# Winograd block products in a decoder layer: the products of a pair summed inside three PSUM banks, neighbouring pairs interleaved, left factors split three products ahead

## The chip, the cores and the metric

The kernel runs on one core of one Trainium2 chip. The metric is the device time of one execution in microseconds; the time before is the median of three executions, 2488.87 us (2486.42 to 2490.97). Five engines work side by side, each through its own queue of instructions in order: PE (matrix products), DVE (vector operations), ACT (activations, copies and casts), POOL (GpSimd, elementwise here) and SP, which issues the DMAs. PE writes into PSUM, which is used in banks of 128 partitions by 512 f32.

## The reference

One layer of a decoder trunk, sequence 1024, width 1024, all in f32:

```python
h = rmsnorm(x, norm_mix)
u = h @ w_in            # dq dk dv | rq rk rv rg | lx ly | gates
od = rmsnorm(diff_attention(dq, dk, dv, lam), diff_subln) * (1 - lam_init)
o_r = silu(rg) * group_norm(retention(rq, rk, rv))
o_l = rg_lru_branch(lx, ...) * gelu(ly)      # conv of 4, two gates, a scan over time
g = sigmoid(gates)                           # three gates of 1024 channels
merged = g0*(od @ w_branch0) + g1*(o_r @ w_branch1) + g2*(o_l @ w_branch2)
x = x + merged @ w_out
x = x + cross_attention(rmsnorm(x), rmsnorm(mem))
x = x + square(relu(rmsnorm(x) @ mlp_w1)) @ mlp_w2
return rmsnorm(x)
```

## The kernel before

**Arithmetic.** Every f32 product is made of three PE products of a faster 32-bit format. An operand is a `Split`: `hi`, a cast by ACT (line 70), and `lo`, the rest, a subtraction by DVE or POOL (line 71). `mm3` (lines 59 to 61) then multiplies hi by hi, hi by lo and lo by hi into the same bank.

**Block products.** The large projections use Winograd's form for 2 x 2 blocks: seven products instead of eight. A *unit* is a [128, 1024] piece of weights, read as a left factor of two blocks; two units make a *pair*, a left factor of 2 x 2 blocks A11 A12 A21 A22, whose result is a block of 256 channels by 1024 rows. Of it come the left factors A11, A12, S4, A22, S1, S2, S3 (`left`, line 1067, four DVE subtractions or additions of 128x512 a pair), and of the activations the right factors B11, B21, B22, T4, T1, T2, T3 (T1 to T4 are kept in DRAM and loaded as *blocks* of [128, 4, 512], each in two halves that ACT and DVE or POOL split). Product k is 12 matmuls of 128x512 into one bank. The seven are combined by `product`: with P1 to P7 the banks, c11 = P2 + P1, u2 = P6 + P1, u3 = P7 + u2, c22 = P5 + u3, u4 = P5 + u2, c21 = P4 + u3, c12 = P3 + u4. A copy of P1 by ACT (line 1122) and seven DVE additions that read a bank (lines 1126, 1128, 1131 for the inner ones, `emit` for the four results) do that, with `t0` and `t1` in SBUF as places for the partial sums.

**Stages.** `h_products` (about 765 to 1302 us) makes 23 pairs with h, the normalised input: eight for the LRU (every second pair), four for retention's gate, eleven for the merge gates. Beside each second pair run the LRU's own steps: a convolution on DVE, two small gate products on PE, sigmoids, tanh, exp and sqrt on ACT, a product on POOL, a scan on DVE. Then three branches (1302 to about 1556 us) of four pairs each, whose results are multiplied by the gates (`sgb`, loaded and put through a sigmoid by ACT) and added to what the branch before left in DRAM (`pv`). While the last two pairs of a branch run, the right factors of the next are loaded into the places that come free. After w_out and the cross-attention, `mlp_in` (about 1820 to 2144 us) makes 16 pairs with a squared ReLU on each result and sums for the next product, and `mlp_out` ends the layer.

**Order.** The Tile framework puts each engine's instructions into an order by the program's text and their dependencies. The text's order of products within a pair is `ORDER` or, where the right factors are still arriving, `BY_BLOCK` with two pairs side by side:

```python
ORDER = (1, 2, 6, 7, 5, 4, 3)
BY_BLOCK = (1, 2, 3, 7, 6, 5, 4)
```

A unit is cast and its low part subtracted where its product stands in the text; four weight tiles (two units each) let this run ahead. Low parts go to POOL, in the branches to DVE for products 6 and 4. PSUM has two banks for general use (`ps`) and six that rotate through the block products.

## Time and profile before

| | us |
|---|---|
| median of three executions | 2488.87 |
| the profiled execution: span | 2489.1 |
| PE busy in it | 2355.3 |
| DVE, ACT, POOL busy | 1851.9, 1042.4, 1088.3 |

The page gives no other time for the profiled execution than its span, which lies 0.2 us above the median. A matmul's row in the trace shows when it starts, how long it took and, in brackets, how long PE had been idle before it and which instruction ended the wait; the releaser named is the instruction whose signal came last. A busy PE is not always PE at full speed: PEclk is the granted clock, 1.00 at full speed.

### The profile page before, as it was taken

What the parts mean: (1) busy time and instruction counts of PE and PEld (TensorE: products, weight loads), DVE (VectorE), ACT (ScalarE), POOL (GpSimd) and SP (SyncE); (2) the same over time, 40 slices, a digit from 0 to 9 for tenths busy, and PEclk for the clock granted to TensorE, in tenths of its full rate; (3) what the DMA queues carried; (4) which work ended last, traced back from release to release, by engine and by line L of the source; (5) the groups of instructions that cost most, each with busy time, mean ns of one, the idle gap of its engine ahead of it and who ended that gap; (6) DMA issues with size and microseconds to landing.
All of it is one profiled execution on the core that took longest, in us unless ns stands there. A gap on an engine that the chain in (4) does not pass through costs nothing. (4 is left out here: it accounts for less than half of the span.)

```text
span 2489.1 us, 31236 instructions
## 1 busy us (share of the span) xinstructions
PE 2355.3 (95%) x11132; PEld 1906.0 (77%) x11132; DVE 1851.9 (74%) x2850; ACT 1042.4 (42%) x1823; POOL 1088.3 (44%) x714
## 2 busy tenths in 40 slices
PE   9999999999999999999998978899989999999996
PEld 7888878787876877777776767688768888778884
DVE  7577476767786777777677887534788888878888
ACT  5443344545455554454354443235442222343333
POOL 1122212221214555565553333225145555698787
PEclk9999999999999999999999989999999999999999
DMA  5222212122114435534576776434225444744432
GB/s 173 74 85 69 62 45 60 44 60 54 51 41 140 152 120 185 182 119 144 194 233 220 241 264 205 141 129 136 94 85 178 148 140 140 275 152 169 147 142 75
DMA packets 137259, 334.08 MB, mean 134 GB/s; under 512 B 17152, under 2 KB 27393, under 8 KB 137104
## 3 DMA queue, kind: packets, MB, share of 16 engines
q1 hardware_dynamic: 136528, 330.25, 40.2%
q8 instruction: 89, 1.46, 0.3%
q10 hardware_dynamic: 576, 1.84, 0.2%
q14 instruction: 66, 0.54, 0.1%
HBM read 229.21 MB, written 98.63 MB: 132 GB/s over the span
## 5 line engine op out<-in xcount | busy, mean ns | idle before, releaser
L59 PE MATMUL ps<-block,wu 128*128 128x512 f32 x1428 | 570.5, 400 | 55.6 <-DVE sf L1126 23.5
L61 PE MATMUL ps<-block,wu 128*128 128x512 f32 x1428 | 568.2, 398 | 16.7 <-POOL wu L71 10.2
L60 PE MATMUL ps<-block,wu 128*128 128x512 f32 x1428 | 565.0, 396 | 0.1
L71 POOL TENSOR_TENSOR wu<-st,wu 128x512 fp32r<-128x512 f32 x214 | 324.9, 1533 | 323.4 <-ACT wu L70 323.3
L59 PEld LDWEIGHTS ps<-block,wu 128*128 128x128 f32 x1428 | 273.2, 191 | 120.0 <-issue 19.6
L61 PEld LDWEIGHTS ps<-block,wu 128*128 128x128 f32 x1428 | 272.9, 191 | 85.5 <-POOL wu L71 15.8
L60 PEld LDWEIGHTS ps<-block,wu 128*128 128x128 f32 x1428 | 272.7, 191 | 60.7 <-DVE block L71 1.1
L70 ACT CAST wu<-st 128x512 fp32r<-128x512 f32 x240 | 141.5, 618 | 163.3 <-DVE st L1067 68.9
L59 PE MATMUL ps<-wu,hu 128*128 128x512 f32 x448 | 176.6, 394 | 15.6 <-DVE acc L1199 13.6
L71 POOL TENSOR_TENSOR w<-st,w 128x1024 fp32r<-128x1024 f32 x50 | 122.1, 2453 | 154.9 <-ACT w L70 137.5
L61 PE MATMUL ps<-wu,hu 128*128 128x512 f32 x448 | 174.9, 392 | 5.1 <-DVE hu L71 5.1
L60 PE MATMUL ps<-wu,hu 128*128 128x512 f32 x448 | 175.2, 391 | 0.1
L1199 DVE TENSOR_TENSOR acc<-acc,ps 128x512 f32<-128x512 f32 x216 | 137.8, 677 | 21.3 <-PE ps L61 20.6
L71 POOL TENSOR_TENSOR wu<-sf,wu 128x512 fp32r<-128x512 f32 x63 | 115.9, 1853 | 64.9 <-ACT wu L70 51.8
L71 DVE TENSOR_TENSOR hu<-sth,hu 128x1024 fp32r<-128x1024 f32 x56 | 122.1, 2185 | 20.6 <-ACT hu L70 20.2
L467 ACT ACTIVATE p<-sc,mx 128x256 f32<-128x256 f32 (+7 forms) x128 | 94.5, 740 | 65.8 <-DVE mx L464 61.9
L59 PEld LDWEIGHTS ps<-wu,hu 128*128 128x128 f32 x448 | 84.6, 189 | 38.9 <-DVE acc L1199 10.7
L59 PE MATMUL psk<-block,w 128*128 128x512 f32 x256 | 104.8, 409 | 0.0
L61 PEld LDWEIGHTS ps<-wu,hu 128*128 128x128 f32 x448 | 84.6, 189 | 23.5 <-DVE hu L71 6.0
L61 PE MATMUL psk<-block,w 128*128 128x512 f32 x256 | 101.8, 398 | 0.0
L60 PE MATMUL psk<-block,w 128*128 128x512 f32 x256 | 101.6, 397 | 0.0
L60 PEld LDWEIGHTS ps<-wu,hu 128*128 128x128 f32 x448 | 84.6, 189 | 17.8 <-POOL wu L71 0.5
(391 smaller groups left out, 5627.2 us busy)
## 6 DMA issues: line engine op xcount, KB each, us to landing
sth<-h SPq DMA_DIRECT2D x56, 512.0 KB, 8.9
st<-in_w SPq DMA_DIRECT2D x32, 512.0 KB, 4.3
h<-hab SPq DMA_DIRECT2D x32, 512.0 KB, 2.8
w<-in_w SPq DMA_DIRECT2D x8, 2048.0 KB
sgb<-gsp SPq DMA_DIRECT2D x48, 256.0 KB, 4.3
gsp<-l SPq DMA_DIRECT2D x44, 256.0 KB, 3.1
acc<-y SPq DMA_DIRECT2D x40, 256.0 KB, 4.2
st<-in_w_br SPq DMA_DIRECT2D x18, 512.0 KB, 6.4
```

What stands on the lines that cost most here:

```text
L59: nc.tensor.matmul(ps, lhsT=lhs.hi, rhs=rhs.hi, start=start, stop=False)
L60: nc.tensor.matmul(ps, lhsT=lhs.hi, rhs=rhs.lo, start=False, stop=False)
L61: nc.tensor.matmul(ps, lhsT=lhs.lo, rhs=rhs.hi, start=False, stop=stop)
L70: ins = self.nc.scalar.copy(dst.hi, src)
L71: self.lo_ins = (lo_engine or self.nc.vector).tensor_tensor(dst.lo, src, f32(dst.hi), op=ALU.subtract)
L467: nc.scalar.activation(p[:, 0:n], sc[:, 0:n], AF.Exp, bias=mx, accum_out=l)
L1199: eng.tensor_tensor(acc[k][:, st, :], acc[k][:, st, :], x if isinstance(x, bass.AP) else acc[x][:, st, :], op=ALU.add)
```

## The change

Three banks serve a pair: X for products 1 and 2, Y for 6, 7 and 4, Z for 5 and 3. A product can start on top of what its bank holds (`onto`: no matmul of it carries `start`). So c11 stands in X after product 2, c21 in Y after product 4 and c12, less one term, in Z after product 3. What is still added by other engines: DVE adds `t0` into bank Y in place after product 6 (u2), ACT copies that to `t0`, ACT copies Y after product 7 to `t1` (u3), and DVE makes c22 = Z + t1 and, at the end, c12 = Z + t0. Results that need no addition are taken from the bank by ACT (Copy, Gelu, Silu, or Relu and Square) or, in the branches, by the DVE multiplication with the gate.

`SLOT` interleaves neighbouring pairs: on PE the products follow one another as 6, 2, 5, 7, then 1 of the next pair, 4, 3, then 6 of the next pair. `play` makes a product's left factor (cast, low part, left sums) three products before it, with the low parts on GpSimd except in the first two pairs of the MLP, which keep the old form as `product_apart`. The left sums are made in place (S2 over A11, S3 over A21, S4 over A12). The two LRU gate products now come after products 4 and 3 of the following pair, both in the `ps` banks. In the branches the addition of `pv` goes from DVE to GpSimd. The right factors are loaded in another order: in `h_products` T2, T1, T3, T4 instead of T3, T2, T1, T4, with T2 needed after product 2 of the first two pairs (before, T3 after their product 3).

```diff
-    ORDER = (1, 2, 6, 7, 5, 4, 3)
-    BY_BLOCK = (1, 2, 3, 7, 6, 5, 4)
+    ORDER = (1, 6, 2, 5, 7, 4, 3)
+    SLOT = {1: 0, 6: 3, 2: 4, 5: 5, 7: 6, 4: 8, 3: 9}
+    BANK = {1: "X", 2: "X", 6: "Y", 7: "Y", 4: "Y", 5: "Z", 3: "Z"}
+    def overlapped(self, pairs):
+        return [x[1:] for x in sorted((7 * p + s, p, k) for p in pairs for k, s in self.SLOT.items())]
+    def play(self, seq, prep, run, ahead=3):
+        for i in range(-ahead, len(seq)):
+            if i + ahead < len(seq):
+                prep(*seq[i + ahead])
+            if i >= 0:
+                run(*seq[i])
...
+    def left_part(self, k, c, eng):
+        w, tt = c["w"], lambda o, x, y, op: eng.tensor_tensor(o, x, y, op=op)
         if k == 1:
+            tt(c["s1"], w["A21"], w["A22"], ALU.add)
+            w["S1"], w["S2"], w["S3"] = c["s1"], w["A11"], w["A21"]
+            tt(w["S3"], w["A11"], w["A21"], ALU.subtract)
+            tt(w["S2"], c["s1"], w["A11"], ALU.subtract)
+        elif k == 2:
+            w["S4"] = w["A12"]
+            tt(w["S4"], w["A12"], w["S2"], ALU.subtract)
...
+    def prepare(self, k, c, lo):
+        c["u", k] = self.pair_unit(c["w"][self.LEFT[k]], lo)
+        self.left_part(k, c, self.nc.vector)
...
+    def product(self, k, c, right, psum, emit, apart=False):
         nc, v = self.nc, self.nc.vector
+        u, r, b = c["u", k], right[self.RIGHT[k]], self.BANK[k]
+        onto = b in c
+        if not onto:
+            c[b] = psum()
+        ps = c[b]
+        self.mmk(ps, [(u[:, kt, :], r[:, kt, :]) for kt in range(4)], onto)
+        t0, t1 = c["t"]
+        if k == 1:
+            nc.scalar.copy(t0, ps)
+            if apart:
+                del c[b]
+        elif k == 2:
+            emit(0, 0, ps, None if onto else t0)
+        elif k == 6:
+            v.tensor_tensor(ps, ps, t0, op=ALU.add)
+            nc.scalar.copy(t0, ps)
+        elif k == 7:
+            nc.scalar.copy(t1, ps)
+            emit(1, 1, c["Z"], t1)
+        elif k == 4:
+            emit(1, 0, ps, None)
+        elif k == 3:
+            emit(0, 1, ps, t0)
...
 # h_products
+        def prep(p, k):
+            load(p)
+            self.prepare(k, cs[p], nc.gpsimd)
+            if k == 6:
+                load(p + 1)
...
-                elif k == self.ORDER[6]:
-                    self.lru_gate(jobs[p - 1][1], cs[p - 1], sp, sps)
+                elif k in (4, 3):
+                    self.lru_gate(jobs[p - 1][1], cs[p - 1], sp, k == 3)
...
-        for i in (3, 2, 1, 4):
+        for i in (2, 1, 3, 4):
...
-        for k in self.BY_BLOCK[1:]:
-            for p in range(2):
-                run(p, k)
-        for p in range(2, m - 2):
-            for k in self.ORDER:
-                run(p, k)
+        self.play([(p, k) for k in (2, 6, 5, 7, 4, 3) for p in range(2)] + self.overlapped(range(2, m - 2)), prep, run)
...
 # branch
-            v.tensor_tensor(o, x, y, op=ALU.add)
-            v.tensor_tensor(o, o, sg, op=ALU.mult)
+            if y is not None:
+                z = x if (n % 2, j) == (0, 1) else o
+                v.tensor_tensor(z, x, y, op=ALU.add)
+                x = z
+            v.tensor_tensor(o, x, sg, op=ALU.mult)
             if order > 0:
-                v.tensor_tensor(o, o, pv, op=ALU.add)
+                nc.gpsimd.tensor_tensor(o, o, pv, op=ALU.add)
...
+        seq = self.overlapped(range(2))
+        seq.insert(seq.index((1, 4)), (2, 1))
+        self.play(seq + [(p, k) for k in self.ORDER for p in (2, 3) if (p, k) != (2, 1)], prep, run)
...
 # mlp_in, emit
+            if y is None:
+                nc.scalar.activation(o, x, AF.Relu)
+                nc.scalar.activation(o, o, AF.Square)
+            else:
+                tt(o, x, y)
+                v.scalar_tensor_tensor(o, o, 0.0, o, op0=ALU.max, op1=ALU.mult)
```

How the instructions move is seen best at three places.

**ACT in one of the LRU's cycles (the sixth of eight), first before, then of the change.** `r` and `g` are the gates; the tanh (line 636 before, 641 after) waits for POOL's product `xc`; exp is line 637 (642 after), sqrt 638 (643); `COPY sf<-ps` of line 1122 is the copy of P1, those of lines 1179 and 1181 are the copies of bank Y after products 6 and 7.

```order
L634 ACT_TABLE_LOAD
L634 ACTIVATE r<-psr,vec 128x512 x2
L634 ACTIVATE g<-psi,vec 128x512 x2
L70 CAST wu<-st 128x512 x2
L1122 COPY sf<-ps_10637 128x512
L636 ACTIVATE g<-r,sp_8517 128x1024
L70 CAST lw<-lws 128x256
L637 ACT_TABLE_LOAD
L637 ACTIVATE r<-r,spm_8518 128x1024
L638 ACT_TABLE_LOAD
L638 ACTIVATE g<-g 128x1024
```

```order
L637 ACTIVATE g<-psr,vec 128x512 x2
L72 CAST wu<-st 128x512 x2
L72 CAST lw<-lws 128x256
L641 ACTIVATE g<-r,sp_8607 128x1024
L72 CAST wu<-st 128x512
L642 ACT_TABLE_LOAD
L642 ACTIVATE r<-r,spm_8608 128x1024
L643 ACT_TABLE_LOAD
L643 ACTIVATE g<-g 128x1024
L1179 COPY sf<-ps_10602 128x512
```

In the sixth, seventh and eighth cycle of the change the copy of line 1179, which product 7 needs, stands behind the sqrt; in the five cycles before, it stands ahead of the tanh, and the copy of line 1181 stands behind the sqrt instead.

**DVE while the second branch's right factors arrive, first before, then of the change.** `block<-st` is the low part of a half block, `wu` that of a unit, `L1126` and `L1178` are u2.

```order
L71 TENSOR_TENSOR block<-st_12401,block 128x1024
L71 TENSOR_TENSOR block<-st_12405,block 128x1024
L71 TENSOR_TENSOR wu<-st,wu 128x512
L71 TENSOR_TENSOR block<-st_12449,block 128x1024
L71 TENSOR_TENSOR wu<-sf,wu 128x512
L71 TENSOR_TENSOR block<-st_12453,block 128x1024
L1067 TENSOR_TENSOR sf<-st 128x512
L1067 TENSOR_TENSOR st<-st 128x512
L1067 TENSOR_TENSOR st<-sf,st 128x512
L1126 TENSOR_TENSOR sf<-ps_12499,sf 128x512
```

```order
L73 TENSOR_TENSOR block<-st_12245,block 128x1024
L73 TENSOR_TENSOR block<-st_12249,block 128x1024
L1178 TENSOR_TENSOR ps_12257<-ps_12257,sf 128x512
L1178 TENSOR_TENSOR ps_12274<-ps_12274,sf 128x512
L73 TENSOR_TENSOR block<-st_12290,block 128x1024
L845 TENSOR_TENSOR y<-ps_12171,sgb 128x512
L73 TENSOR_TENSOR block<-st_12294,block 128x1024
```

u2 stood behind six half blocks of this load and now stands behind two; no low part of a unit is left between them.

**ACT at the same place, of the change.** The casts of the half blocks wait for their DMAs; product 4 of the last two pairs waits for the two copies of line 1181. Before, the only copies here were those of P1.

```order
L72 CAST block<-st_12340 128x1024
L72 CAST block<-st_12344 128x1024
L836 ACTIVATE sgb<-sgb 128x512 x2
L72 CAST block<-st_12380 128x1024
L1181 COPY sf<-ps_12257 128x512
L72 CAST block<-st_12384 128x1024
L1181 COPY sf<-ps_12274 128x512
```

The first copy stands behind the seventh half block of the load, the second behind the eighth.

More of the change, by code (lines that the diff above doesn't have):

```diff
@@ L688, in emit @@
                     g = self.gate_order[n + i]
-                    tt(o[:, 0:HB], x, y)
+                    out(o[:, 0:HB])
                     nc.sync.dma_start(self.gsp[g * P:(g + 1) * P, sl], o[:, 0:HB])
@@ L722, in h_products, with last @@
                 self.after("hdma", nc.sync.dma_start(st, self.hTs[i - 1][:, 2 * q:2 * q + 2, :]))
-                self.split(b[:, 2 * q:2 * q + 2, :], st, nc.gpsimd if q and i != 3 else v)
-        for k in self.BY_BLOCK[1:]:
-            for p in range(2):
-                run(p, k)
-        for p in range(2, m - 2):
-            for k in self.ORDER:
-                run(p, k)
-        tags = itertools.cycle("rg")
-        self.right, load = self.load_blocks(1, lambda: self.sp.tile([P, 2, HB], F32, tag=next(tags), name="sto"))
-        for k in self.BY_BLOCK:
-            for p in range(m - 2, m):
-                run(p, k)
-            next(load)
+                self.split(b[:, 2 * q:2 * q + 2, :], st, nc.gpsimd if q and i != 2 else v)
+        self.play([(p, k) for k in (2, 6, 5, 7, 4, 3) for p in range(2)] + self.overlapped(range(2, m - 2)), prep, run)
+        tags = itertools.cycle("rg")
+        self.right, blocks = self.load_blocks(1, lambda: self.sp.tile([P, 2, HB], F32, tag=next(tags), name="sto"))
+        def last(p, k):
+            run(p, k)
+            if p == m - 1:
+                next(blocks)
+        self.play([(p, k) for k in self.ORDER for p in range(m - 2, m)], prep, last)
+    SLOT = {1: 0, 6: 3, 2: 4, 5: 5, 7: 6, 4: 8, 3: 9}
[7 more added lines that the diff above has]
+                run(*seq[i])
     def p6(self, psum):
```

189 lines of the change are left out of this document (102 added, 87 removed).

## The prediction

> **What bounds the kernel now.** I read the engines' shares first, then PE's waits by stage, then the stages by windows, and only then single rows. The page's first part says that PE is busy nearly all the time:
>
> ```profile
> PE 2355.3 (95%) x11132; PEld 1906.0 (77%) x11132; DVE 1851.9 (74%) x2850; ACT 1042.4 (42%) x1823; POOL 1088.3 (44%) x714
> ```
>
> So 134 us of idle PE are all there is to win, beside matmuls that run at less than full clock. The windows (length, then busy time and count of PE, PEld, DVE, ACT, POOL, then the granted clock, the DMA share and GB/s) show where they lie: h_products, the branches, three stretches within those or their ends, and the MLP's first product.
>
> ```profile
> 804.00:1302.00 498.00, 471.62 (x2000) 379.06 (x1999) 369.26 (x403) 232.09 (x334) 285.43 (x181) 0.98 0.50 167
> 1302.00:1556.00 254.00, 222.13 (x930) 179.59 (x929) 203.91 (x249) 111.60 (x171) 87.83 (x56) 0.94 0.70 230
> 1434.00:1538.00 104.00, 88.03 (x365) 70.71 (x363) 86.14 (x106) 45.98 (x70) 34.19 (x21) 0.93 0.75 247
> 1920.00:2100.00 180.00, 180.00 (x787) 147.40 (x786) 151.07 (x177) 41.35 (x74) 100.05 (x66) 1.00 0.45 152
> 1290.00:1300.00 10.00, 10.00 (x45) 8.23 (x44) 7.34 (x7) 5.06 (x8) 3.10 (x3) 1.00 0.94 323
> ```
>
> PE idles 498.00 - 471.62 = 26.4 us in h_products and 254.00 - 222.13 = 31.9 us in the branches; in the MLP window, which uses the same block products, it never idles. PE's waits, first in h_products, then in the branches:
>
> ```profile
> PE ps L59 <- DVE sf L1131: 13.3, 6, 2.6
> PE ps L61 <- POOL wu L71: 9.6, 12, 1.7
> PE ps L59 <- DVE sf L1126: 2.7, 1, 2.7
> ...
> PE ps L59 <- DVE sf L1126: 20.8, 3, 10.2
> PE ps L59 <- ACT wx L70: 5.9, 1, 5.9
> ```
>
> Two things are late: DVE with the additions that empty a bank, and the low part of a left factor. One such wait, on PE and on DVE:
>
> ```profile
> 930.12 0.40 PE L61 MATMUL ps<-block,wu 128*128 128x512 f32 x1
> 933.13 0.47 PE L59 MATMUL ps<-block,wu 128*128 128x512 f32 x1 [2.61 <-DVE sf L1131]
> 933.81 0.63 PE L61 MATMUL ps<-block,wu 128*128 128x512 f32 x1
> 934.24 0.63 PE L59 MATMUL ps<-block,wu 128*128 128x512 f32 x1
> ```
>
> ```profile
> 926.85 3.38 DVE L641 TENSOR_TENSOR_SCAN g<-r,xc 128x1024 f32<-128x1024 f32 x1
> 932.30 0.68 DVE L1131 TENSOR_TENSOR sf<-ps,sf 128x512 f32<-128x512 f32 x1
> ```
>
> The LRU's scan stood ahead of the addition; the bank came free 2.6 us late, and the matmuls after it start 0.43 us apart. Undisturbed ones do this:
>
> ```profile
> 783.77 0.39 PE L59 MATMUL ps<-block,wu 128*128 128x512 f32 x1
> 788.98 0.39 PE L61 MATMUL ps<-block,wu 128*128 128x512 f32 x1
> 793.44 1.16 PE L59 MATMUL ps<-block,wu 128*128 128x512 f32 x2 [4.08 <-ACT block L70]
> ```
>
> The first two rows are the first and last of 24 matmuls: 5.21 / 23 = 0.2265 us from start to start, so a product of twelve takes 2.72 us. Summed over all such slow matmuls, the low clock costs 7.5 us in h_products and 8.0 in the branches, 1.2 us per long wait. In all 33.9 and 39.9 us are lost there.
>
> **The change part by part.** The sum is made against the profiled execution's 2489.1 us; the median is 0.2 less.
>
> *Opening of h_products.* The third row above is PE waiting for the first T block. Its load is issued where it was, but only products 1 and 2 of two pairs come ahead of it, not 1, 2 and 3: 2 x 2.72 = 5.4 us less cover. **+5.4** (0 if the load moves up with the shorter stage before it, 8 if the second block is late too).
>
> *Additions taken off DVE, low parts earlier.* Per pair four of seven additions at 0.68 us go, 2.7 us of a pair's 19; banks are held by pairs, but six of them serve two pairs, and a unit made three products ahead has 8.2 us for cast (0.62) and low part (1.55). The 33.9 us of waits in h_products should go. What comes is a chain inside bank Y. The durations:
>
> ```profile
> L71 POOL TENSOR_TENSOR wu<-st,wu 128x512 fp32r<-128x512 f32 x113 | 173.2, 1552 | 122.0 <-ACT wu L70 121.8
> L70 ACT CAST wu<-st 128x512 fp32r<-128x512 f32 x115 | 66.6, 618 | 69.1 <-DVE st L1067 55.6 <-PE ps L61 6.9 <-DMA st<-in_w_gate 6.5
> L635 POOL TENSOR_TENSOR xc<-g,xc 128x1024 f32<-128x1024 f32 x8 | 19.2, 2402 | 28.6 <-ACT g L634 28.6
> L1122 ACT COPY sf<-ps 128x512 f32<-128x512 f32 x22 | 12.9, 586 | 5.9 <-PE ps L61 5.9
> L637 ACT ACT_TABLE_LOAD x8 | 10.3, 1283 | 0.1
> L634 ACT ACTIVATE g<-psi,vec 128x512 f32<-128x512 f32 x16 | 10.1, 689 | 3.7 <-DMA oTs<-g 2.1 <-PE ps L61 1.7
> L637 ACT ACTIVATE r<-r,spm 128x1024 f32<-128x1024 f32 x8 | 9.2, 1154 | 0.1
> L636 ACT ACTIVATE g<-r,sp 128x1024 f32<-128x1024 f32 x8 | 9.2, 1153 | 9.4 <-POOL xc L635 9.4
> L638 ACT ACTIVATE g<-g 128x1024 f32<-128x1024 f32 x8 | 8.5, 1063 | 0.1
> ```
>
> Between 6 and 7 lie two products, 5.4 us, for DVE's addition and ACT's copy. The addition into a bank is not in the trace; below, it takes the 0.68 us of an addition that reads one, above, four times the in-place one over 128 columns:
>
> ```profile
> L462 DVE TENSOR_TENSOR sc<-sc,cm x128: 268/298/300, 304.9 to 758.9; 128x128 f32<-128x128 f32 x128
> ```
>
> that is 1.2 us; I take 0.68, whose shape is the same. With 0.59 for the copy the chain fits, unless an engine is held up. ACT is, once per LRU cycle. I count from the end of product 4. The gates' 12 matmuls with product 3 between end at 5.4, the last sigmoid at 6.1. In cycles six to eight the order puts one cast (6.7) and its low part (8.3) ahead of POOL's product (10.7); then tanh (11.9), a cast (12.5), table and exp (14.9), table and sqrt (17.3), and only then the copy (17.9). Product 7 could start at 5.4 + 3 x 2.72 = 13.6: it waits 4.3 us and loses 1.2 to the clock, 5.5 x 3 = **16.5**. In the other five the copy after 6 is ahead of the tanh, and POOL's product has no late low part ahead of it: it ends at 8.5, tanh at 9.7, table and Gelu at 11.6, sqrt at 16.3, the copy after 7 at 16.9, with 19.0 allowed. That holds with 2.1 us to spare; I charge 1 each, **5**, since POOL may be in the middle of a low part. At the last pairs ACT also casts the first branch's half blocks, as it does between branches:
>
> ```profile
> 1336.38 2.00 ACT L70 CAST block<-st 128x1024 fp32r<-128x1024 f32 x2
> 1357.57 1.04 ACT L70 CAST block<-st 128x1024 fp32r<-128x1024 f32 x1 [2.55 <-DMA st<-oTs]
> 1360.63 1.05 ACT L70 CAST block<-st 128x1024 fp32r<-128x1024 f32 x1 [1.49 <-DMA st<-oTs]
> ```
>
> These are half blocks 1 and 2, 7 and 8. The first can start 5.4 us into the last two pairs (after both products 1); the seventh is then cast at 26.6, the copy of line 1181 behind it ends at 28.2, and product 4 could start after ten products, at 27.2; the eighth delays the second copy by another 0.4: **1.4**. So h_products: -33.9 + 16.5 + 5 + 1.4 = **-11.0** (-29 if only the 5 come, +11 if all eight cycles are late).
>
> *Branches.* The 39.9 us go as far as DVE causes them: u2 stood behind six half blocks, now behind two, and DVE gives up the `pv` additions and the low parts of products 6 and 4. Whether the gate's multiplication from a bank is cheaper, the next rows tell (min/median/max):
>
> ```profile
> L810 DVE TENSOR_TENSOR y<-ps,sf x48: 673/678/692, 1302.2 to 1569.5; 128x512 f32<-128x512 f32 x48
> L811 DVE TENSOR_TENSOR y<-y,sgb x48: 674/681/2875, 1305.3 to 1573.5; 128x512 f32<-128x512 f32 x48
> ```
>
> With a bank as one input it never takes more than 0.69; with two in SBUF up to 2.9. The Trainium skill, "SBUF — State Buffer", section "Who interferes with whom", says why: DVE with two SBUF inputs and GpSimd reading SBUF exclude each other for a whole instruction. These rows agree. The same rule speaks against the change, as it gives GpSimd more to read in SBUF while the left sums stay on DVE; by it the sum would lose some tenths of a us for each such sum, hidden where DVE has time.
>
> POOL's addition of `pv` is not in the trace: half of line 635's 2.40 below, 1.55 above; I take 1.3, so that a branch asks 28 x 1.55 + 16 x 1.3 = 64 us of POOL's 76. Hidden, just. What remains:
> - the wait for `wx` (5.9 and 1.6 of clock), which the change doesn't touch: 7.5;
> - DMA. The middle branch moves 48 pieces of 256 KB and 22 of 512 KB (sizes as the page's last part has them):
>
> ```profile
> sgb<-gsp SPq DMA_DIRECT2D x48, 256.0 KB, 4.3
> acc<-y SPq DMA_DIRECT2D x40, 256.0 KB, 4.2
> st<-in_w_br SPq DMA_DIRECT2D x18, 512.0 KB, 6.4
> ```
>
> that is 24.1 MB in 28 x 2.72 = 76.2 us of PE. Midway between the 247 GB/s of the windows and their 323 at best it takes 84.6: 8.4;
> - two more loads of blocks, 1.4 each: 2.8;
> - copies behind a sigmoid that waits for its `sgb` (63.5 us in 29 waits, 2.2 each, under one product's 2.72):
>
> ```profile
> ACT sgb L805 <- DMA sgb<-gsp: 63.5, 29, 6.9
> ```
>
> A few exceed it; I take 4.
>
> Together 22.7, so **-17.2** (-32 with the `wx` wait alone, +5 where a copy of each pair waits 2.2).
>
> *The rest.* At w_out the blocks last needed now come by way of POOL's additions: 0 (-5 to +5). In the MLP the order puts the end of one pair (an addition of 0.68, a square and a difference) and two left sums ahead of u2 and its copy. At the duration of the square before,
>
> ```profile
> L1155 DVE SCALAR_TENSOR_TENSOR hab<-hab 128x512 f32<-128x512 f32 x63 | 66.1, 1050 | 1.3
> ```
>
> for each of these four, that is 0.68 + 4 x 1.05 + 0.68 + 0.59 = 6.2 us against the 8.2 between products 3 and 7: **+1** (0 to +8). The squares moved to ACT cost nothing there: ACT is busy 41 of 180 us, and without that cover each is 1 us.
>
> Sum: 2489.1 + 5.4 - 11.0 - 17.2 + 1 = **2467**.
>
> **The rivals.**
> *Nearly all of it comes* (0.20). The chains fit everywhere but in cycles six to eight: 2489.1 - 33.9 + 16.5 - 39.9 + 7.5 + 5.4 = **2445**. For it: the MLP window shows these products without a wait. Against it: its ACT has nothing else to do.
>
> *ACT becomes the bound* (0.24), the case on the other side. Bank Y lets PE in only after ACT's copies, and ACT works in order. If all eight LRU cycles lose 5.5 us and one copy of each of the twelve branch pairs waits 2.2, h_products loses 44 + 1.4 - 33.9 = 11.5 and the branches 7.5 + 8.4 + 2.8 + 26.4 - 39.9 = 5.2: 2489.1 + 5.4 + 11.5 + 5.2 + 1 = **2512**. It decides from about 4 us a cycle, if the branches gain nothing. The Trainium skill, "PSUM — Partial Sum Buffer", section "PSUM bank collisions raise a hardware error", speaks for it: accesses of different engines to one bank have to be put one after the other, reads too. The waits of L59 on line 1131 agree for PE and DVE; three engines taking turns in one bank no row here shows.
>
> *DMA holds the branches* (0.18). At the 247 GB/s of the window above the middle branch takes 97.6 us, and the branches keep their 39.9: 2489.1 + 5.4 - 11.0 + 1 = **2484**, no change.
>
> The forecast has 0.38. **Chances:** a difference under 0.2%, 5 us, can't be told from none. Faster: 0.36 of the forecast, 0.20, and 0.06 of the DMA case, 0.62; the same 0.12, mostly the DMA case; slower 0.26. The range of 2440 to 2503 leaves out the tails of the second and third case, a tenth on each side; the forecast's own is 2455 to 2482.
>
> **What would show it.** Opening: the first wait on a T block near 9.5 us. h_products: no wait on line 1178 or on a low part; three waits of some 4 us of the `onto` matmuls on ACT's copies. Branches: PE's wait for `wx` left, DVE's long ones gone, GB/s near 285. Wrong would be the forecast if ACT's copies head PE's list of waits, or if DVE's left sums, now waiting for POOL's low parts, hold up u2.

## The result, and the profile after

The changed kernel takes 2550.92 us (median of four runs, 2549.82 to 2551.91) against 2487.64 us for the kernel before on the same chip: a ratio of 1.0257 [1.0242, 1.0271]. It is **slower by 2.6%**, where 2467 us were forecast. Its profiled execution spans 2549.6 us, 60.5 more than the one before. The engines' shares of the kernel after:

```profile
PE 2377.0 (93%) x11132; PEld 1918.0 (75%) x11132; DVE 1683.7 (66%) x2572; ACT 1155.0 (45%) x2016; POOL 1143.5 (45%) x770
```

DVE gave up 168 us of work, as the change says, and the number of matmuls is the same. PE still idles 39 us more, and its busy time rose by 22 us, which for equal matmuls points to more of them at the lower clock. To see where, I cut both traces at the same events: ACT's copy of P1 of the third, the 23rd and the 24th pair (the 24th is the first pair of the branches), the first matmul of w_out, the first of `mlp_out`, and the end of the span. All stage times below are cut this way, in us, from one trace of each kernel; where no edit touches a stage, two traces differ by up to 1.7 between the third and the 23rd pair, and by up to 4.2 in the branches (255.7 to 259.9 in seven versions with the same branches).

| | to the third pair | third to 23rd | 23rd to 24th | branches | w_out to `mlp_in` | `mlp_out` |
|---|---|---|---|---|---|---|
| before | 826.3 | 422.5 | 41.9 | 265.5 | 587.5 | 345.4 |
| after | 829.2 | 470.3 | 46.0 | 278.6 | 588.3 | 337.1 |
| difference | +2.9 | +47.8 | +4.1 | +13.1 | +0.8 | -8.3 |

So two stages lose and one gains. PE's waits over the whole kernel after, the longest of that list first:

```profile
PE ps L59 <- ACT sf L1179: 38.3, 10, 7.4
PE ps L59 <- ACT sf L1181: 31.2, 14, 7.2
PE ps L59 <- DVE acc L1293: 14.3, 10, 3.3
PE ps L59 <- ACT sf L1172: 13.6, 4, 6.7
```

Line 1179 is ACT's copy of bank Y after product 6 (product 7 may not start before it), line 1181 the copy after product 7 (product 4 waits for it), line 1172 the copy of P1 (product 2 waits for it). ACT's copies head the list, which the prediction had named as a sign that it is wrong. The windows of the two stages that lose, before:

```profile
826.00:1249.00 423.00, 399.31 (x1684) 319.93 (x1684) 310.38 (x342) 197.65 (x285) 240.21 (x154) 0.98 0.46 154
1290.00:1556.00 266.00, 234.13 (x982) 189.46 (x981) 213.25 (x256) 118.63 (x180) 92.93 (x59) 0.94 0.71 235
```

and after:

```profile
829.00:1300.00 471.00, 415.34 (x1696) 330.73 (x1697) 284.29 (x263) 245.39 (x358) 244.11 (x158) 0.94 0.41 139
1345.00:1624.00 279.00, 242.72 (x984) 193.75 (x985) 155.83 (x159) 129.12 (x202) 158.77 (x108) 0.93 0.68 220
```

In h_products (the first row of each) PE idles 55.7 us instead of 23.7, and the granted clock falls from 0.98 to 0.94: 94 matmuls run at about half pace instead of 38, 20.0 us of extra time instead of 7.5. Idle 32.0 and clock 12.5 together are 44.5 of the 47.8. DMA moves less per second, not more, in both stages, so its rate isn't the bound. In the branches POOL is busy 158.8 us instead of 92.9.

**One wait in full.** In the kernel after, PE (the last matmul of product 5, then product 7 of the same pair):

```profile
1056.17 0.40 PE L61 MATMUL ps<-block,wu 128*128 128x512 f32 x1
1061.92 0.79 PE L59 MATMUL ps<-block,wu 128*128 128x512 f32 x1 [5.36 <-ACT sf L1179]
1062.51 0.63 PE L60 MATMUL ps<-block,wu 128*128 128x512 f32 x1
1062.94 0.63 PE L61 MATMUL ps<-block,wu 128*128 128x512 f32 x1
```

ACT, which had been idle for 2.54 us when its copy came:

```profile
1061.28 0.59 ACT L1179 COPY sf<-ps 128x512 f32<-128x512 f32 x1 [2.54 <-DVE ps L1178]
```

and DVE, ahead of its addition into the bank (line 1178, u2):

```profile
1047.34 3.38 DVE L646 TENSOR_TENSOR_SCAN g<-r,xc 128x1024 f32<-128x1024 f32 x1
1051.85 1.76 DVE L1125 TENSOR_TENSOR st<-sf,st 128x512 f32<-128x512 f32 x1 [1.12 <-POOL wu L73]
1053.54 1.75 DVE L647 TENSOR_TENSOR l<-l,g 128x1024 f32<-128x1024 f32 x1
1055.21 1.78 DVE L616 TENSOR_SCALAR xc<-lx,vec 128x1024 f32<-128x1024 f32 x1
1056.91 0.68 DVE L689 TENSOR_TENSOR l<-ps,sf 128x512 f32<-128x512 f32 x1
1057.51 1.27 DVE L618 SCALAR_TENSOR_TENSOR xc<-lx,vec,xc 128x1024 f32<-128x1024 f32 x1
1058.71 0.68 DVE L780 TENSOR_TENSOR r<-r 128x512 f32<-128x512 f32 x1
1059.31 1.27 DVE L618 SCALAR_TENSOR_TENSOR xc<-lx,vec,xc 128x1024 f32<-128x1024 f32 x1
1060.50 0.69 DVE L1178 TENSOR_TENSOR ps<-ps,sf 128x512 f32<-128x512 f32 x1
```

Product 6 had ended two products, 5.4 us, before product 5 did, so near 1051.1. Its addition began 9.4 us later. Before it stood a left sum that waited 1.12 us for POOL, the LRU's product, three steps of the next convolution, a result (line 689) and a sum for a branch's input (line 780): all of them DVE's own work in its own order. The addition took 0.69 us and the copy 0.59. ACT was not what was late here; it merely came last in the chain, and the list of waits names the last.

The chain is PE, DVE, ACT, PE, inside one bank, with 5.4 us of cover. Before, the same addition could be late by more, since it freed a bank of its own and PE had others to go on with.

**The eight waits taken apart.** In h_products PE waits eight times for line 1179, 33.1 us in all, once per LRU cycle. The first five, 29.1 us (4.9 to 7.4 each), are of the kind just shown: ACT had been idle before its copy until the addition ended, and the same left sum, product, convolution steps, result and branch sum stood ahead of the addition, which began 8.9 to 11.4 us after product 6. In cycles six to eight DVE is in time and ACT is late, as here in the sixth (PE, DVE, ACT):

```profile
1138.88 0.50 PE L59 MATMUL ps<-block,wu 128*128 128x512 f32 x1 [1.08 <-ACT sf L1179]
```

```profile
1131.41 0.70 DVE L1178 TENSOR_TENSOR ps<-ps,sf 128x512 f32<-128x512 f32 x1 [1.96 <-PE ps L61]
```

```profile
1137.30 1.06 ACT L643 ACTIVATE g<-g 128x1024 f32<-128x1024 f32 x1
1138.26 0.57 ACT L1179 COPY sf<-ps 128x512 f32<-128x512 f32 x1
```

The copy stands behind the sqrt and comes 6.1 us after the addition. These three waits are 1.1, 1.6 and 1.3 us, 4.0 in all. In the other five cycles PE also waits 0.7 to 1.2 us, 4.7 in all, for the copy of line 1181, again behind ACT's sqrt. So ACT is late where the prediction put it and costs little there; DVE is late where the prediction charged nothing.

### The profile page after: what moved, and what is told of

Same layout as the page of the kernel before. It is cut to its first block, busy times and chain, and to the rows that moved or that the text cites. A ratio compares the mean times of both kernels' runs of the same rounds, so it can differ in the third digit from the quotient of the medians.

```text
span 2549.6 us, 30999 instructions
## 1 busy us (share of the span) xinstructions
PE 2377.0 (93%) x11132; PEld 1918.0 (75%) x11132; DVE 1683.7 (66%) x2572; ACT 1155.0 (45%) x2016; POOL 1143.5 (45%) x770
## 5 line engine op out<-in xcount | busy, mean ns | idle before, releaser
L59 PE MATMUL ps<-block,wu 128*128 128x512 f32 x1428 | 583.3, 409 | 113.4 <-ACT sf L1179 38.3
L61 PE MATMUL ps<-block,wu 128*128 128x512 f32 x1428 | 573.8, 402 | 0.9 <-DVE wu L73 0.5
L60 PE MATMUL ps<-block,wu 128*128 128x512 f32 x1428 | 572.6, 401 | 0.0
L73 POOL TENSOR_TENSOR wu<-st,wu 128x512 fp32r<-128x512 f32 x232 | 353.3, 1533 | 360.3 <-ACT wu L72 348.7
L59 PEld LDWEIGHTS ps<-block,wu 128*128 128x128 f32 x1428 | 277.7, 195 | 190.4 <-ACT sf L1179 42.7
L61 PEld LDWEIGHTS ps<-block,wu 128*128 128x128 f32 x1428 | 277.4, 194 | 67.1 <-DVE wu L73 0.9
L60 PEld LDWEIGHTS ps<-block,wu 128*128 128x128 f32 x1428 | 278.1, 195 | 61.8 <-DVE block L73 0.8
L59 PE MATMUL ps<-wu,hu 128*128 128x512 f32 x448 | 176.1, 393 | 14.3 <-DVE acc L1293 14.3
L1125 DVE TENSOR_TENSOR st<-st 128x512 f32<-128x512 f32 x69 | 87.7, 1272 | 78.7 <-POOL wu L73 77.8
L73 POOL TENSOR_TENSOR wu<-sf,wu 128x512 fp32r<-128x512 f32 x69 | 108.8, 1584 | 45.6 <-ACT wu L72 34.0
L59 PEld LDWEIGHTS ps<-wu,hu 128*128 128x128 f32 x448 | 84.4, 188 | 36.2 <-DVE acc L1293 13.3
L61 PEld LDWEIGHTS ps<-wu,hu 128*128 128x128 f32 x448 | 84.6, 189 | 19.0 <-DVE hu L73 1.3
```

What stands on the lines that cost most here:

```text
L59: nc.tensor.matmul(ps, lhsT=lhs.hi, rhs=rhs.hi, start=start, stop=False, **kw)
L60: nc.tensor.matmul(ps, lhsT=lhs.hi, rhs=rhs.lo, start=False, stop=False, **kw)
L61: nc.tensor.matmul(ps, lhsT=lhs.lo, rhs=rhs.hi, start=False, stop=stop, **kw)
L73: self.lo_ins = (lo_engine or self.nc.vector).tensor_tensor(dst.lo, src, f32(dst.hi), op=ALU.subtract)
L1125: w, tt = c["w"], lambda o, x, y, op: eng.tensor_tensor(o, x, y, op=op)
```

## The experiments

Stage times of all runs (cut as above; the first column of the table above stayed within 826.1 and 831.0, that of w_out to `mlp_in` within 581.5 and 599.9, the longest in e1 to e4, whose edits reach the MLP too), with the ratio to the kernel before. "Own banks" means that no sum is made in a bank: every product has its own, and the additions are DVE's, as before.

| run | third to 23rd | 23rd to 24th | branches | `mlp_out` | ratio [95%] |
|---|---|---|---|---|---|
| before | 422.5 | 41.9 | 265.5 | 345.4 | 1 |
| after | 470.3 | 46.0 | 278.6 | 337.1 | 1.0257 [1.0242, 1.0271] |
| e1, own banks everywhere | 449.1 | 44.1 | 283.7 | 342.9 | 1.0230 [1.0188, 1.0272] |
| e2, bank Y alone undone | 461.7 | 42.5 | 282.7 | 335.3 | 1.0265 [1.0232, 1.0298] |
| e3, ACT's copies to DVE | 472.3 | 42.9 | 280.8 | 336.4 | 1.0273 [1.0233, 1.0314] |
| e4, factors one product ahead | 474.9 | 44.4 | 274.0 | 337.7 | 1.0281 [1.0248, 1.0314] |
| x8, before with the new MLP | 423.2 | 42.7 | 265.7 | 336.8 | 0.9964 [0.9946, 0.9982] |
| x5, gates as before, `pv` on DVE | 467.9 | 44.4 | 264.8 | 337.7 | 1.0158 [1.0128, 1.0187] |
| x6, x5 with own banks in h_products | 444.0 | 41.0 | 263.8 | 336.8 | 1.0049 [1.0027, 1.0072] |
| x7, x6 in the old order | 428.0 | 40.5 | 259.4 | 337.2 | 0.9947 [0.9916, 0.9979] |
| z2, after with one tap of the convolution | 464.5 | 43.9 | 279.6 | 337.9 | 1.0218 [1.0185, 1.0250] |
| y3, x6 with factors five ahead | 452.0 | 41.2 | 260.5 | 336.7 | 1.0051 [1.0031, 1.0071] |
| x9, x7 with before's h_products | 423.8 | 43.4 | 258.2 | 337.5 | 0.9939 [0.9918, 0.9960] |
| y7, x7 with the gates' input split earlier | 419.6 | 41.7 | 258.0 | 337.5 | 0.9923 [0.9899, 0.9948] |
| i1, y7 interleaved | 442.2 | 41.2 | 255.7 | 336.8 | 1.0007 [0.9996, 1.0017] |
| w1b, y7 with products 1, 6, 2, 7, 5, 4, 3 | 421.7 | 41.8 | 259.0 | 337.8 | 0.9943 [0.9921, 0.9966] |
| w1, w1b with the sums in banks | 452.5 | 42.4 | 259.0 | 337.9 | 1.0077 [1.0046, 1.0107] |
| w2, w1b with bank X's sum alone | 424.1 | 41.4 | 259.9 | 337.6 | 0.9942 [0.9925, 0.9958] |
| w3, after with `pv` on DVE | 468.6 | 45.8 | 262.1 | 337.6 | 1.0172 [1.0142, 1.0201] |
| w4, y7 with `pv` on GpSimd | 420.2 | 42.9 | 268.9 | 336.7 | 0.9964 [0.9947, 0.9981] |

### Parts undone in the changed kernel

Four runs undo one suspect each. e1 takes all sums out of the banks:

```diff
-            self.product(k, c, H, psum or self.p6(sps), emit, psum is not None)
+            self.product_apart(k, c, H, psum or self.p6(sps), emit)
```

(and the same in the branches and the MLP). 

> The change with every product in a bank of its own again and all sums made by DVE as before the change; order, interleaving, splitting three ahead and the additions on GpSimd stay. Theory A (the chain in one bank: product 6, DVE's addition, ACT's copy, product 7, ACT's copy, product 4 lets PE wait for the queues of DVE and ACT): the waits on those copies, 76 us in the block products, go, some of the old waits for a bank (16 to 24 us) come back; 2470 to 2500 us. Theory B (splitting ahead with the low parts on GpSimd and sums in place makes DVE wait and collide): DVE has even more to do, 2540 us or more. Theory C (weights loaded later, so that DVE waits for them): little moves, 2530 to 2560.

e2 gives products 7 and 4 banks of their own, so that only the chain of bank Y goes:

```diff
-    BANK = {1: "X", 2: "X", 6: "Y", 7: "Y", 4: "Y", 5: "Z", 3: "Z"}
+    BANK = {1: "X", 2: "X", 6: "Y", 7: "U", 4: "V", 5: "Z", 3: "Z"}
-            v.tensor_tensor(ps, ps, t0, op=ALU.add)
-            nc.scalar.copy(t0, ps)
+            v.tensor_tensor(t0, ps, t0, op=ALU.add)
-            nc.scalar.copy(t1, ps)
+            v.tensor_tensor(t1, ps, t0, op=ALU.add)
...
-            emit(1, 0, ps, None)
+            emit(1, 0, ps, t1)
```

> The change with bank Y alone undone: products 6, 7 and 4 have a bank each and DVE adds as before (u2, u3, c21); banks X and Z still sum in place. Theory A: as PE waits on nothing between 6, 7 and 4, nearly all of the 70 us of waits on the copies after 6 and 7 go, and DVE's load stays under that of before: 2460 to 2490 us. Theory B or C: 2530 us or more.

e3 leaves the chain and takes ACT's queue out of it, at the price of two more copies in DVE's queue:

```diff
-            nc.scalar.copy(t0, ps)
+            v.tensor_copy(t0, ps)
-            nc.scalar.copy(t1, ps)
+            v.tensor_copy(t1, ps)
```

> The change with the copies after products 6 and 7 made by DVE instead of ACT; everything else as it is. Theory A says which queue holds which copy: in the branches the copy after 7 waits behind ACT's sigmoids and casts that wait for DMAs (27 us of PE's waits there), and these go, in h_products the copy after 6 waits for DVE's addition behind the LRU's scan and convolution, and those 33 us stay: 2510 to 2535 us. If ACT's queue were the bound in both places, 2470 to 2490. If neither, 2550 or more.

e4 splits the left factors one product ahead instead of three (`ahead=1`). 

> The change with left factors split one product ahead instead of three. Theory A: the chain is unchanged and low parts come late again (10 us of waits before the change): 2550 to 2590 us. Theory B: DVE waits less for GpSimd between its sums, and the time falls to 2530 us or less.

Between the third and the 23rd pair e1 gave back 21.2 us, e2 8.6, e3 nothing (+2.0) and e4 nothing (+4.6). As whole kernels e1, e2 and e3 (2541.6, 2550.2 and 2552.2 us) stay above the ranges that theory A, the chain alone, gave them. The sums in the banks are part of the loss; the distance of three isn't. e3 alone doesn't clear ACT's queue: with the copies on DVE, PE waits 22.0 us for line 1181, where it was 4.7. That DVE and not ACT makes most of the waits shows in the eight taken apart above. e1 got less than half of what was lost, and its waits show why. PE's waits in h_products of e1:

```profile
PE psr L59 <- ACT r L637: 29.7, 6, 8.7
PE psr L60 <- DVE xcs L73: 8.3, 3, 4.1
```

With the bank chain gone, PE waits where it hadn't: for the LRU gates (`psr`), whose products the change had put at another place, and for the low part of their input. In the kernel after, these two waits hid behind the others. So one limit taken away at a time undercounts each, and I went on from the other end.

### The change taken apart, from the old kernel's side

x8 is the kernel before with the MLP's part of the change alone. x5 is the changed kernel with the LRU gates where they were and `pv` added by DVE; x6 is x5 with own banks in h_products (and the branches' low parts of products 6 and 4 on DVE again); x7 is x6 with the old order of products and loads and the split of the gates' input after product 4, where it stood, and in the branches own banks and all low parts on GpSimd. In short:

```diff
# x5, against the changed kernel
-                elif k in (4, 3):
-                    self.lru_gate(jobs[p - 1][1], cs[p - 1], sp, k == 3)
+                elif k == 3:
+                    self.lru_gate(jobs[p - 1][1], cs[p - 1], sp, sps)
-                nc.gpsimd.tensor_tensor(o, o, pv, op=ALU.add)
+                v.tensor_tensor(o, o, pv, op=ALU.add)
# x6, against x5
-            self.product(k, c, H, psum or self.p6(sps), emit, psum is not None)
+            self.product_apart(k, c, H, psum or self.p6(sps), emit)
-            self.prepare(k, cs[p], nc.gpsimd)
+            self.prepare(k, cs[p], v if k in (6, 4) else nc.gpsimd)
# x7, against x6
-    ORDER = (1, 6, 2, 5, 7, 4, 3)
+    ORDER = (1, 2, 6, 7, 5, 4, 3)
-        for i in (2, 1, 3, 4):
+        for i in (3, 2, 1, 4):
...
```

> Two edits of the change, in stages that the trace separates. In h_products the LRU's two gate products go back to where they were before the change (both after product 3, the second one's banks from the rotating six); the sums stay in the banks. In the branches the addition of pv goes back to DVE. Own banks took 21 us of the 52 lost in h_products, and then PE waited for the gates' products instead (38 us, for ACT's sigmoids and the low part of their input). Theory D (two limits that hide each other, the chain in bank Y and the gates' place): this edit alone moves h_products by less than 10 us. Theory E (the gates' place is the main loss, by making the LRU's own chain longer): it gives 25 us or more. Branches: if GpSimd's additions make its low parts late, 5 to 13 us come back; if the stream of blocks from DRAM is the limit, under 3 us.

> In h_products both are undone, the sums in the banks and the gates' place; the interleaving, the splitting three ahead and the left sums in place stay. Theory D: most of the loss goes, the stage of h_products is within 10 us of before. If it still loses 20 us or more, the interleaving or the splitting ahead is a cause of its own. In the branches the addition of pv is on DVE and the low parts of products 6 and 4 are on DVE, as before the change, with the sums in the banks: as in the run beside it, 5 to 13 us come back if GpSimd's load is the cause, under 3 us if it isn't.

> In h_products and the branches the order of products, the order of loads and the places of the gates and of the LRU's steps go back to before the change, each product has its own bank and pv is added by DVE; what is left of the change there is the splitting three products ahead with the left sums in place and all low parts on GpSimd. The MLP is that of the change. If the interleaving and the sums in the banks are the causes, both stages are back within 8 us of before, 2475 to 2492 us in all (the MLP's part gained 8). If splitting ahead is a cause, 2505 us or more.

> The kernel before with the change in the MLP's first product alone. In the change's trace the stages from w_out on took 8 us less than before, at the start of the MLP's second product, and the first product's own time is the same. If that gain belongs to the MLP's part: 2476 to 2483 us, that is 5 to 10 us faster than before. If it came from elsewhere, no change.

The gates' place is worth 2.4 us in h_products (470.3 to 467.9), hardly more than traces differ (w3, below, has the h_products of the kernel after and 468.6), the sums in banks 23.9 (x5 to x6), and the rest lies in x6 to x7, 16.0, where several edits stand together. x8 shows that the MLP's part is a gain by itself: h_products and the branches as before, `mlp_out` 8.6 us shorter. In the branches x5 and x6 stand at 264.8 and 263.8, so the low parts of products 6 and 4 matter no more there.

### Is it DVE's queue, and are the weights late?

If u2 is late because of what stands ahead of it on DVE, then less of that should help. z2 is the changed kernel with three of the four taps of the LRU's convolution left out (`range(1, 4)` to `range(1, 1)`), so part of the reference's work is missing there. 

> The change with three of the four taps of the LRU's convolution left out: eight times 3 x 1.3 = 3.9 us less on DVE, of which two taps (2.6 us) stand between the LRU's scan and the u2 addition into bank Y. Everything else is the change. Theory A' (in h_products PE's wait for the copy after product 6 is DVE's queue: scan, convolution, left sums ahead of u2): these eight waits, 33 us, shrink by 2.6 each and the slow matmuls after them with them; the stage from the third to the 23rd pair falls by 20 to 35 us, 2515 to 2532 in all. If ACT's queue or the gates set it, under 8 us: 2542 or more.

```profile
PE ps L59 <- ACT sf L1179: 20.6, 8, 4.4
PE ps L59 <- DVE lx L689: 10.4, 3, 4.9
PE psr L59 <- ACT r L637: 9.7, 3, 3.3
```

That is PE's list in h_products of z2. The first row was 33.1 us in eight waits in the kernel after, so 12.5 went, and all of it from the five waits behind DVE: they fell from 29.1 to 16.7 us, by 2.2 to 3.0 each, where two taps are 2.6. The three behind ACT stayed (4.0 and 3.9). This shows DVE's queue in those five waits. But the stage gained only 5.8, which by what was expected speaks for another bound: the wait for the gates (`psr`) rose from 2.2 to 9.7, again one limit behind another.

y3 asks whether x6's interleaved order suffers from weights that come late: five products ahead instead of three. 

> The run with the gates' place, the banks (h_products) and the pv addition undone, but the factors made five products ahead instead of three. There the interleaved order is what is left against the run with the old order (16 us in h_products), and DVE waits 36 us for LRU weights, against 5. Theory C (interleaving keeps the stage tiles longer, so the next weights come late and DVE waits for them): made two products earlier, the tiles come free 5 us sooner, DVE's waits for weights fall by half and h_products by 5 us or more. If not, no change or slower, and the weights are not the cause.

DVE's waits for the LRU's weights went from 35.7 to 31.5 us and the stage got 8 us slower. Earlier splitting is no cure; as the waits hardly fell, it doesn't tell what they cost.

x9 and y7 put together the parts that helped. x9 is x7 with the h_products of before; y7 is x7 with one line moved:

```diff
-                if k == 4:
+                if k == 7:
                     self.lru_split(...)
```

> The h_products of the kernel before, with the branches of the run with the old order (own banks, factors three ahead, pv on DVE) and the MLP of the change. By stages: h_products 422.5 against 428.0 in that run, branches 259.4 against 265.5 before, from the MLP's second product 8 less: 2463 to 2475 us, faster than both kernels.

> The run with the old order, with the split of the gates' input two products earlier in the text (after product 7 instead of 4). There PE waits 26 us, seven times, for that split's low part on DVE. If the place in DVE's and ACT's queues is the cause, most of that goes: 2450 to 2466 us. If the convolution before it ends late, nothing changes: 2470 to 2480 us.

In x7 PE waited 26.4 us for the low part of the gates' input. y7 splits that input two products earlier, and the stage falls from 428.0 to 419.6, less than was expected. y7 is the fastest version: 2470.84 us, 0.9923 [0.9899, 0.9948] of the kernel before. It keeps the splitting three products ahead with the low parts on GpSimd, the earlier split of the gates' input and the MLP of the change, and drops the rest. x9, which has the old h_products and the same branches and MLP, lies at 0.9939 [0.9918, 0.9960], too near to tell the two apart by their times alone.

### Each part alone, from the fastest version

y7 is a base without either suspect, so each can be added singly. i1 adds the interleaving in h_products:

```diff
-        ... + [(p, k) for p in range(2, m - 2) for k in self.ORDER], prep, run)
+        ... + self.overlapped(range(2, m - 2)), prep, run)
```

> The fastest kernel (own banks, old order, gates' split early) with one edit: in h_products the pairs from the third to the 21st are interleaved as in the change. If interleaving costs by itself, as the run with own banks and the change's order suggests (444 against 420 us from the third to the 23rd pair): 438 us or more, with DVE waiting 30 us or more for weights. If it was the place of the other steps there: 425 or less.

w1b is y7 with the order 1, 6, 2, 7, 5, 4, 3 within a pair (still not interleaved), w1 the same with the sums in the banks, and w2 with that of bank X alone (product 2 on top of P1; nothing but ACT's copy of P1 between them):

```diff
# w1, against w1b
-            self.product_apart(k, c, H, psum or self.p6(sps), emit)
+            (self.product_s if 1 < p < m - 2 else self.product_apart)(k, c, H, psum or self.p6(sps), emit)
# w2, in product_x
+        ps = c[1] if k == 2 else psum()
...
+        if ready("c11", 2, "u1"):
+            emit(0, 0, c[2], None)
```

> The fastest kernel so far (old order, own banks, factors three ahead, pv on DVE, the gates' split early) with the sums of h_products back in three banks from the third pair on, and no interleaving of pairs: within a pair 1, 6, 2, 7, 5, 4, 3, so that one product lies in each link of the chain. If the sums in the banks cost by making PE wait for DVE's and ACT's queues, whatever the order: h_products from the third to the 23rd pair 440 us or more, against 420, with the waits on the copies after products 6 and 7. If it is interleaving alone: 425 or less.

> The run beside it with own banks, in the same order within a pair. It is the one that the other is compared with: 418 to 426 us for that stage, since only the order within a pair differs from the fastest kernel's.

> The fastest kernel with one sum in a bank in h_products: product 2 on top of product 1, with product 6 between them, so that c11 is taken from the bank by ACT and DVE has one addition less a pair. PE waits only for ACT's copy of P1, with 2.7 us to do it, and no DVE step is in that chain. If the loss of the sums in the banks is DVE's place in the chain: no loss here, 2462 to 2476 us. If any wait of PE for a copy costs: 2480 or more.

The two suspects cost, each by itself, between the third and the 23rd pair: interleaving 442.2 - 419.6 = **22.6**, the sums in the banks 452.5 - 421.7 = **30.8** (there with one product between 6 and 7; with two, x5 against x6, **23.9**). The order within a pair, with own banks, is worth 2.1 at most (421.7 against 419.6). The waits of PE in w1, in h_products:

```profile
PE ps L59 <- ACT sf L1204: 27.3, 17, 4.0
PE ps L59 <- ACT sf L1197: 13.6, 6, 4.8
```

and in w1b:

```profile
PE ps L59 <- DVE sf L1210: 12.1, 6, 2.8
```

Line 1204 of w1 is the copy after product 6, line 1197 that of P1, line 1210 of w1b a DVE addition that frees a bank. Where the additions free a bank, PE waits 12.1 us for them; where the sums are links of a chain, it waits 27.3 + 13.6 = 40.9 for the copies. Of the 17 waits on line 1204, nine, 18.9 us, have ACT idle until DVE's addition ended; in the other eight, 8.5 us, ACT's own queue holds the copy. Bank X alone, where no DVE step is in the chain, costs 2.4 us in the stage, and its interval is nearly that of w1b: PE waits 25.3 us for the copy of P1, but its other waits go, and from 826 to 1250 it idles 22.4 us where w1b has 26.1. Banks Y and Z were not added singly, and w1 also takes results from the banks by ACT, so the split of the 30.8 between them stays open.

What interleaving costs by itself shows on DVE. DVE's waits for weights in h_products of y7:

```profile
DVE sf L1121 <- DMA st<-in_w_gate: 7.8, 3, 6.1
DVE sf L1121 <- DMA st<-in_w_lru: 5.9, 7, 1.7
```

and of i1:

```profile
DVE sf L1121 <- DMA st<-in_w_lru: 32.6, 7, 8.3
DVE sf L1121 <- DMA st<-in_w_gate: 14.3, 2, 8.7
```

PE idles 37.4 us of this stage in i1 and 25.0 in y7. Why the weights come later isn't shown: the staging tiles of the pair before may still be held, but the load of 973.87 us in i1, for which DVE waited 5.2, was issued right behind stores that themselves waited for DVE. Nor is it shown that the waits cause the 22.6 us: y3, which was to shorten them, hardly did. More staging tiles were not tried. This cause **stays open**; its size doesn't.

### The branches

w3 is the changed kernel with `pv` added by DVE and nothing else, w4 is y7 with `pv` added by GpSimd:

```diff
-                nc.gpsimd.tensor_tensor(o, o, pv, op=ALU.add)
+                v.tensor_tensor(o, o, pv, op=ALU.add)
```

> The change with the addition of pv in the branches back on DVE, and nothing else. In the run that had this edit and another in h_products, the branches took 13.8 us less. If it is this edit: the branches' stage 263 to 268 us against 278.6, 2534 to 2541 us in all. If GpSimd's additions are not the cause: 275 or more.

> The reverse in the fastest kernel: the addition of pv on GpSimd. If GpSimd's place in the queue of the low parts is what costs, whatever the order of the products: the branches' stage goes from 258 to 268 us or more. If it costs only together with the sums in the banks: under 262.

That one line is worth 278.6 - 262.1 = 16.5 us of the branches in the changed kernel and 268.9 - 258.0 = 10.9 in y7. The groups and waits of the kernel after, in the branches:

```profile
L847 POOL TENSOR_TENSOR y<-y,pv 128x512 f32<-128x512 f32 x29 | 42.2, 1461 | 36.3 <-DVE y L845 26.0 <-issue 10.3
...
PE ps L59 <- ACT sf L1181: 25.6, 7, 7.2
PE ps L59 <- ACT sf L1172: 10.6, 3, 6.7
```

and of w3:

```profile
L847 DVE TENSOR_TENSOR y<-y,pv 128x512 f32<-128x512 f32 x28 | 30.6, 1094 | 0.6
...
PE ps L59 <- ACT sf L1181: 12.1, 7, 3.6
PE ps L59 <- ACT sf L1172: 9.6, 3, 7.4
```

The addition takes 1.46 us on POOL and 1.09 on DVE. The price is not the problem. POOL waits 26.0 us, up to 8.6 at a time, for DVE's product `y` (line 845), with the low parts of the next left factors behind it in its queue. On DVE the two follow each other at once (0.6 us of idle time in all). But POOL's waits can't be all of it: in w4 POOL waits only 4.9 us for `y`, and the move costs 10.9. What both pairs of runs have is a store that waits longer on SP's queue, with loads behind it: SP waits 57.0 us for POOL's additions before the stores of `y` in the kernel after and 33.7 for DVE's in w3, 49.9 in w4 and 33.8 in y7.

The wait for line 1181 halves mainly by two waits, 7.22 and 6.97 us in the kernel after, 1.11 and 1.60 in w3, both for a copy behind the cast of a half block. The longer one, on POOL, SP, ACT and PE:

```profile
1496.72 2.28 POOL L847 TENSOR_TENSOR y<-y,pv 128x512 f32<-128x512 f32 x1
```

```profile
1499.03 0.32 SPq L849 DMA_DIRECT2D acc<-y  x1
1500.41 0.38 SPq L806 DMA_DIRECT2D st<-oTs  x1
```

```profile
1507.12 1.04 ACT L72 CAST block<-st 128x1024 fp32r<-128x1024 f32 x1 [3.21 <-DMA st<-oTs]
1508.08 0.58 ACT L1181 COPY sf<-ps 128x512 f32<-128x512 f32 x1
```

```profile
1508.71 0.80 PE L59 MATMUL ps<-block,wu 128*128 128x512 f32 x1 [7.22 <-ACT sf L1181]
```

POOL's addition stood behind two low parts, the store waited 3.9 us for it, the load of the half block was issued behind the store, and ACT waited for that load before it came to the copy. In w3 the load was issued at 1494.96, and PE waited 1.11. One wait followed so far doesn't show that the whole 10.9 to 16.5 us come this way.

## Why the prediction was wrong

**Opening** (+5.4 forecast). PE waited for the first T block 7.27 us, before 4.08; the cut at the third pair is 2.9 later. The mechanism was right, the size a little too big (3.2 us more of wait).

**h_products** (-11.0 forecast; +47.8 and +4.1 measured). The step that failed is "With 0.59 for the copy the chain fits, unless an engine is held up. ACT is, once per LRU cycle". I counted what stands ahead of ACT's copy and not what stands ahead of DVE's addition, though the wait that I had quoted from before, behind the scan, was DVE's, and though the last sentence named DVE's left sums as a sign, without a price. The term for DVE was nothing, without a reason; in the five cycles that I took for the easier ones it measured 29.1 us. ACT's own lateness came at the places forecast and was overpriced: three waits of 1.1 to 1.6 us where 4.3 each were forecast, five of 0.7 to 1.2 where 1 each was charged. The two prices inside the chain were right: 0.694 us median for the addition into the bank, 0.59 for the copy. The sums in banks cost 24 to 31 us, where ACT's lateness was to cost 21.5 and to be paid out of the 33.9; that the two sums are near each other is chance, as the engine is another. Second, interleaving was costed at nothing and costs 22.6. Third, "the 33.9 us of waits in h_products should go": even y7, with low parts three products ahead and own banks, idles 25 us there, against 23.7 before:

```profile
826.00:1246.00 420.00, 394.98 (x1684) 317.78 (x1683) 317.00 (x342) 198.47 (x285) 248.59 (x157) 0.99 0.46 156
...
PE ps L59 <- DVE sf L1210: 14.1, 7, 2.6
PE ps L59 <- DVE sf L1207: 8.4, 5, 2.0
PE ps L61 <- POOL wu L73: 1.6, 2, 1.4
```

The 9.6 us of waits for low parts did fall, to 1.6, as forecast; in their place PE waits longer for the additions that empty a bank, 22.5 us where it was 13.3 (both from 826 to 1250). The one relief went into the next wait. The pieces add up: 419.6 + 22.6 for interleaving = 442.2, x6 has 444.0; + 23.9 for the banks = 467.9; + 2.4 for the gates' place = 470.3.

**Branches** (-17.2 forecast, +13.1 measured). The failed step is "a branch asks 28 x 1.55 + 16 x 1.3 = 64 us of POOL's 76. Hidden, just". 1.3 was near the 1.46 measured. But a share of busy time says nothing of order: POOL's additions wait for DVE inside an in-order queue, and this move costs 10.9 to 16.5 us. Without it the branches stand at 262.1, 3.4 less than before and within what traces differ. There the copies of line 1181 behind sigmoids and casts, charged 4, still cost PE 12.1 us of waits; of the 9.6 for the copy of P1, 7.4 are one wait at the start, behind the cast of a half block that waited 6.7 us for its DMA. Of the two changes of branch, forecast at 1.4 each, the first held (PE waited 0.80 us for line 1181 behind a block's cast), the second didn't (7.22; 1.11 in w3). The forecast of more GB/s was wrong: 220.

**MLP** (+1 forecast). To the end of `mlp_in` it is +0.8: there the chain in the banks does fit, and PE waits only 3.5 us for line 1179. `mlp_out` gains 8.3, which I had not foreseen; x8 shows that it belongs to the MLP's part. PE's waits there before were 13.6 us for line 1199, 5.1 for `hu` and 1.8 for `hab`; after, 14.3 for the same additions (line 1293) and 0.8 for `hu`, 5.4 us less; the rest of the 8.3 I can't place.

**The rivals.** "ACT becomes the bound", 2512, had the sign and the place: all eight cycles wait, as PE's list in h_products of the kernel after has it:

```profile
PE ps L59 <- ACT sf L1179: 33.1, 8, 7.4
```

It had the wrong engine in five of the eight, 29.1 of the 33.1 us, and it was 39 us short, as it knew nothing of interleaving and `pv`. The page that stood beside it, the Trainium skill, "PSUM — Partial Sum Buffer", section "PSUM bank collisions raise a hardware error", on engines put one after the other in a bank, agrees with w1, where product 7 shares a bank with ACT's copy and PE waits 27.3 us for it, and with w1b, where it has its own and that wait is gone. That DMA's rate holds the branches is not borne out: it fell, from 235 GB/s to 220, as the stage got longer.

## What to carry to other kernels

A sum moved into a PSUM bank turns an addition that may be late into a link that PE waits for: price its chain against every in-order queue that it passes, the vector engine's other work above all, and not only the engine whose instruction comes last in the list of waits. Work given to a less busy engine is free only if its input is ready when its turn comes and its result is out in time, since what stands behind it waits too, on its own queue and on the queue that issues the store and the loads. When one part undone gives back less than was lost, look for the next limit behind it, and measure the parts again by adding each alone to a version that has none of them.

## What was not expected of the hardware

DVE's left sums of two SBUF operands, the same instruction in the same number, took much longer in the kernel after (minimum, median, maximum in ns), before and after:

```profile
L1067 DVE TENSOR_TENSOR st<-st x69: 675/693/1785, 767.1 to 2104.7; 128x512 f32<-128x512 f32 x69
```

```profile
L1125 DVE TENSOR_TENSOR st<-st x69: 674/1680/1796, 767.2 to 2182.3; 128x512 f32<-128x512 f32 x69
```

This is what the Trainium skill, "SBUF — State Buffer", section "Who interferes with whom", would have happen where they run beside GpSimd's subtractions, and the trace agrees: of the 30 in h_products of the kernel after, all 16 that took over 1.1 us ran while GpSimd was busy, and only 4 of the 14 short ones did. But the total of GpSimd's work in h_products is nearly the same (244.1 us against 240.2), so it is the timing of the two that changed. The prediction had allowed "some tenths of a us" each; it is a whole one for more than half of them. The sums in banks alone don't decide it: the median in h_products is 1.67 to 1.75 us in w1, x5, e4 and the kernel after, but 1.22 in e3 and 0.69 in z2, which have them too, and 0.69 to 1.15 in e1, x6, x7, i1 and w1b, which don't. What puts the two engines in step isn't shown.
